# Reading the moving operand from the last token to the first in a two-layer decoder trunk

## The chip, the core and the metric

The kernel runs on one core of a Trainium2 chip. A core has a matrix engine (TensorE; PE in the profile, with its weight loads as PEld), a vector engine (VectorE, DVE), a scalar engine (ScalarE, ACT), GpSimd (POOL) and a sync engine (SyncE, SP) that here issues most of the DMAs. Data are worked on in an on-chip memory of 128 partitions (SBUF); TensorE writes its products into a second one (PSUM) of eight banks, each of 512 f32 per partition. The metric is the device time of one execution in microseconds; lower is better.

A matmul here has a *stationary* operand, a block of up to 128 x 128 that is loaded into the array by a weight load of its own, and a *moving* operand, which is streamed past it column by column. Each column of the moving operand gives one column of the output.

## What is computed

A trunk of two layers over 256 tokens with 1024 features. Each layer has a SwiGLU feed-forward of half weight, a token mixer (differential attention in the first layer, forgetting attention in the second), and another feed-forward. Before each stands an RMS norm whose shift and scale come from a conditioning vector.

```python
def swiglu(h, w_in, w_out):
    g, u = jnp.split(h @ w_in, 2, axis=-1)
    return (jax.nn.silu(g) * u) @ w_out

for layer in range(DEPTH):
    if layer == N_A_LAYERS:
        k_sh, v_sh, F_sh = shared_kv(x, ...)
    mod = c_act @ ada_w[layer] + ada_b[layer]
    sh1, sc1, g1, sh2, sc2, g2, sh3, sc3, g3 = jnp.split(mod, N_MOD, axis=-1)
    h = modulate(rms_norm(x, norm_g[layer, 0]), sh1, sc1)
    x = x + 0.5 * g1[:, None, :] * swiglu(h, ffn_w_in[layer, 0], ffn_w_out[layer, 0])
    h = modulate(rms_norm(x, norm_g[layer, 1]), sh2, sc2)
    mix = diff_attention(h, ...) if layer < N_A_LAYERS else forgetting_attention(h, ..., k_sh, v_sh, F_sh)
    x = x + g2[:, None, :] * mix
    h = modulate(rms_norm(x, norm_g[layer, 2]), sh3, sc3)
    x = x + 0.5 * g3[:, None, :] * swiglu(h, ffn_w_in[layer, 1], ffn_w_out[layer, 1])
return rms_norm(x, final_g)
```

The hidden width of the feed-forward is 2816. All inputs and outputs are f32.

## The kernel before, in words

The data are kept transposed: features on the partitions, tokens along the free dimension. So nearly every projection is a product whose *weights are stationary* (a block of 128 input features by 128 output features) and whose *moving operand is the data* (128 input features by 256 tokens). The output in PSUM is 128 output features by 256 tokens.

Full f32 accuracy is made from a faster format, f32r, by splitting each number into a high part (the value rounded to f32r) and a low part (what is left). Weights become `wh` and `wl`, data `HH` and `HL` (in the feed-forward's hidden layer `hidh` and `hidl`; in the attentions' outputs `oh`, `ol`, `obh`, `obl`). One product of a 128 x 128 block is then three matmuls into the same place of PSUM: `wh` with the high data, `wl` with the high data, `wh` with the low data. The function `mm3` (L405) issues these three; every projection with stationary weights calls it:

- the up projections of the feed-forwards, with outputs `pf` (the first blocks of the very first one), `pg` and `pu` (gate and up halves);
- the down projections of the first three feed-forwards, output `po`;
- the projections right after a down projection, whose moving operand is 258 columns wide (`SX`, L33): 256 tokens and the columns of the shift, since the norm's factor is not known yet and is multiplied in later (outputs `lp`, `lq`, `lg`, `lu`);
- the queries and keys of the first attention (`pqk`), some keys of the second (`pk`), and the output projections of the attentions (`pw` with `oh`, `ol`, `obh`, `obl`).

Not through `mm3` go the value projections (`pv`, where the data are stationary and the weights move), the down projection of the last feed-forward (`Last.down`, also with moving weights; its output is named `po` too, but its rows name the weights first), the scores, the transposes and the value products of the attentions (`s`, `sb`, `wa`, `wb`, and a small `po`), and the sums of squares of the norms (`psn`, in plain f32).

Weights come from HBM in pieces of 128 x 1024 (`raw`), loaded by SP; ACT rounds each piece to `wh`, and DVE subtracts to get `wl`. The tile of such a piece is 1088 wide (`WB`, L35), and at the first pieces of some stages the piece is put 16 or 32 elements further into it (`shift`, L263 to L270).

The order on each engine is that of the program's text. The class `InOrder` (L54) wraps each engine's calls: it keeps a rough clock of its own for each engine and uses it only to decide, while the program is built, where on ACT and DVE a piece of weights is prepared between other work. To know when an operand is ready, it keys each operand by its tensor's name and, for some tensors, by the offset of the view (L81).

Of the kernel before, what the change touches and what calls it, by code (L numbers as in the profile page):

```python
# [50 lines left out]
V_ADAB = 65  # L51


class InOrder:  # L54


# [18 lines left out]
    def __getattr__(self, name):  # L75
        f = getattr(self.engine, name)

        def call(*args, **kw):
            aps = [v for v in (*args, *kw.values()) if hasattr(v, "tensor")]
            if aps:  # L80
                names = [(v.tensor.name, v.offset if v.tensor.name[:2] in ("HH", "HL", "x_", "mo") else 0) for v in aps]  # L81
                cost = self.fixed + self.rate * math.prod(aps[0].shape[1:])
                if aps[1:] and aps[1].dtype == F32:
                    cost *= {"matmul": 4, "transpose": 2}.get(name, 1)
                start = max(InOrder.ready.get(n, 0.0) for n in names[name == "matmul":])
                if self.fill and not self.busy:
                    self.busy = True
                    self.fill(start)
                    self.busy = False
                self.t = max(self.t, start) + cost  # L90
                if name == "dma_start":
                    InOrder.ready[names[0]] = self.t + 2.0
                else:
                    outs = [names[0]] + ([(kw["accum_out"].tensor.name, 0)] if kw.get("accum_out") is not None else [])
                    for n in outs:
                        InOrder.ready[n] = self.t + 0.06
            else:
                self.t += 1.3
            return self.tc.keep_in_program_order(f(*args, **kw))  # L99
        return call  # L100
# [3 lines left out]
def trunk(ctx, tc, a, out):  # L104
# [243 lines left out]
    def work(cols):  # L348

        credit[0] = min(CREDIT, credit[0] + pace[0] * 2 * cols / 2048)  # L350
        if mode[0] != "hold":
            bg()
# [51 lines left out]

    def mm3(ps, w, xx, first, last):  # L405
        (wh, wl), (xh, xl) = w, xx
        mm(ps, wh, xh, start=first, stop=False, skip_group_check=True)
        mm(ps, wl, xh, start=False, stop=False, skip_group_check=True)
        mm(ps, wh, xl, start=False, stop=last, skip_group_check=True)
        work(P)  # L410


    HH = cp_.tile([P, NC, SP_], F32R, name="HH")
    HL = cp_.tile([P, NC, SP_], F32R, name="HL")
# [89 lines left out]
    def late_pair(src, dst, r, name):  # L504

        banks = [mmbank(f"{name}{b}") for b in range(2)]
        blk = take(src)
        for k in range(NC):
            for b in range(2):
                mm3(banks[b][:, :SX], blk(k * 256 + b * P), hx[k], k == 0, k == NC - 1)  # L510
            if k == NC - 1:
                late_out(dst, banks, r)
            yield k, NC

    def late_pairs(src, dsts, m, then):

        pb = []
        for i in range(2):  # L520
            banks = [mmbank(f"lp{i}{b}") for b in range(2)]
            pb.append(banks)
            blk = take(src)
            for k in range(NC):
                for b in range(2):
                    mm3(banks[b][:, :SX], blk(k * 256 + b * P), hx[k], k == 0, k == NC - 1)
                if i == 0:
                    if k == 3:
                        r = rstd_of(then)
                        mh = MakeH(r, m) if m else None  # L530
                else:
                    if k == 0:
                        late_out(dsts[0], pb[0], r)
                    if mh:
                        mh.go()
        if mh:
            mh.go(9 - mh.k)
        late_out(dsts[1], pb[1], r)
        mode[0] = "run"
        return r  # L540


    def ffn(l, i, kind, m, nxt, at=2):
# [24 lines left out]
        if (l, i) == (0, 0):  # L568
            banks = ([mmbank(f"pf{b}") for b in range(4)] + [sbank(f"pf{b}") for b in range(4, 6)]
                     + [abank("pf6"), bbank("pf7")])  # L570
            for k in range(NC):
                if k:
                    ada_block()
                    cp_part()
                    ada_block()
                f = make_h(k, kind, m)
                sub_part()
                cp_part()
                f()
                sub_part()  # L580
                blk = take("win0")
                for b in range(4 * K0):
                    mm3(banks[b // 2][:, (b % 2) * 256:(b % 2) * 256 + 256], blk(b * P), hn[k],
                        k == 0 and b % 2 == 0, k == NC - 1)
# [915 lines left out]
```

## Time and profile before

| | us |
|---|---|
| median of two runs | 977.47 |
| the two runs | 976.68 and 978.26 |
| span of the profiled execution (first to last instruction) | 974.4 |

The profiled execution's own time is given as its span only; the 3.1 us between the span and the median of the runs lie outside the program's first and last instruction, or in the difference between executions. In the profile an engine's busy time is the union of its instructions' times. A matmul's own duration (276 ns for 256 columns) is longer than the step from one matmul to the next, since matmuls overlap in the array; the pace is read from the starts, or from the length of a stretch divided by the number of matmuls in it. Nearly all instructions carry the line L99, since `InOrder` records them; the tiles' names tell them apart. Out<-in names an instruction's output and inputs.

The DMA queues moved 268.22 MB at 275 GB/s on average; DVE is busy for 818.5 us and ACT for 552.4 us.

### The profile page before, as it was taken

How to read it: one execution, taken by the hardware profiler on the slowest of the kernel's cores; microseconds unless marked ns; L12 is line 12 of the kernel's file. 1: busy time of each engine (PE TensorE's matmuls, PEld its weight loads, DVE VectorE, ACT ScalarE, POOL GpSimd, SP SyncE). 2: the span in 40 equal slices, each digit the busy share in tenths (PEclk: the TensorE clock that was granted, in tenths of full speed). 3: DMA queues.
4: the chain of work that ended last, by engine and by line, in shares of the span. 5: the costliest groups of instructions: out<-in, count | busy, mean ns of one | idle time of the engine just before them, and what ended most of it. 6: DMA issues, size and time to landing. Idle time of an engine off the chain costs nothing.

```text
span 974.4 us, 20491 instructions
## 1 busy us (share of the span) xinstructions
PE 963.7 (99%) x8124; PEld 939.9 (96%) x8124; DVE 818.5 (84%) x1372; ACT 552.4 (57%) x902; POOL 54.6 (6%) x94
## 2 busy tenths in 40 slices
PE   8999999999999999999999999999999999999997
PEld 6999999998999999999997999999998999999997
DVE  7989979989999999878899989989977699555575
ACT  5466545566787645455576554445567576455432
POOL 0000200000112000000000000000011014300000
PEclk9999999999999999999999999999999999999999
DMA  9988999967776699888959899998885337978651
GB/s 360 415 352 279 332 372 339 345 225 272 293 239 232 209 381 370 293 287 314 329 179 370 308 338 337 345 314 319 297 278 174 104 109 228 266 149 276 185 152 44
DMA packets 69473, 268.22 MB, mean 275 GB/s; under 512 B 9417, under 2 KB 10225, under 8 KB 59266
## 3 DMA queue, kind: packets, MB, share of 16 engines
q1 hardware_dynamic: 66016, 259.69, 76.1%
q0 software_dynamic: 3072, 6.92, 2.5%
q8 instruction: 63, 1.03, 0.4%
q10 hardware_dynamic: 290, 0.32, 0.1%
q14 instruction: 32, 0.26, 0.1%
HBM read 264.75 MB, written 2.66 MB: 274 GB/s over the span
## 4 chain that ended last, share of the span: by engine, by line
PE 97%; DVE 1%; DMA 1%; ACT 0%; issue 0%; SPq 0%; DVEq 0%; ACTq 0%
PE po L99 25%; PE pg L99 21%; PE pu L99 21%; PE pf L99 5%; PE pv L99 5%; PE pw L99 4%; PE lp L99 4%; PE pqk L99 3%; PE wb L99 1%; PE lq L99 1%; PE lu L99 1%; PE lg L99 1%; PE pk L99 1%; PE sb L99 1%; DMA ada<-in_ada 1%; PE s L99 1%
## 5 line engine op out<-in xcount | busy, mean ns | idle before, releaser
L99 ACT CAST wh<-raw 128x1024 fp32r<-128x1024 f32 (+1 forms) x360 | 347.3, 975 | 210.8 <-PE pu L99 82.0
L99 DVE TENSOR_TENSOR wl<-raw,wh 128x1024 fp32r<-128x1024 f32 (+1 forms) x360 | 398.6, 1126 | 70.9 <-ACT sg L99 20.3
L99 DVE CUSTOM_DVE_ANT_0 ada<-ada,cact,vecs 128x1024 f32<-128x1024 f32 x160 | 203.6, 1279 | 0.4 <-DMA ada<-in_ada 0.4
L99 PE MATMUL pg<-HH,wh 128*128 128x256 f32 x608 | 168.0, 276 | 0.0
L99 PE MATMUL pg<-HH,wl 128*128 128x256 f32 x608 | 167.9, 276 | 0.0
L99 PE MATMUL pu<-HH,wh 128*128 128x256 f32 x608 | 167.9, 276 | 0.0
L99 PE MATMUL pu<-HL,wh 128*128 128x256 f32 x608 | 167.9, 276 | 0.0
L99 PE MATMUL pg<-HL,wh 128*128 128x256 f32 x608 | 167.9, 276 | 0.0
L99 PE MATMUL pu<-HH,wl 128*128 128x256 f32 x608 | 167.9, 276 | 0.0
L99 PE MATMUL po<-hidh,wh 128*128 128x256 f32 x528 | 145.7, 276 | 0.0
L99 PE MATMUL po<-hidh,wl 128*128 128x256 f32 x528 | 145.7, 276 | 0.0
L99 PE MATMUL po<-hidl,wh 128*128 128x256 f32 x528 | 145.7, 276 | 0.0
L99 PEld LDWEIGHTS pg<-HH,wh 128*128 128x128 f32 x608 | 114.1, 188 | 0.7 <-issue 0.6
L99 PEld LDWEIGHTS pg<-HH,wl 128*128 128x128 f32 x608 | 114.1, 188 | 0.0
L99 PEld LDWEIGHTS pu<-HH,wh 128*128 128x128 f32 x608 | 114.1, 188 | 0.0
L99 PEld LDWEIGHTS pg<-HL,wh 128*128 128x128 f32 x608 | 114.1, 188 | 0.0
L99 PEld LDWEIGHTS pu<-HL,wh 128*128 128x128 f32 x608 | 114.1, 188 | 0.0
L99 PEld LDWEIGHTS pu<-HH,wl 128*128 128x128 f32 x608 | 114.1, 188 | 0.0
L99 PEld LDWEIGHTS po<-hidh,wh 128*128 128x128 f32 x528 | 99.1, 188 | 0.0
L99 PEld LDWEIGHTS po<-hidl,wh 128*128 128x128 f32 x528 | 99.1, 188 | 0.0
L99 PEld LDWEIGHTS po<-hidh,wl 128*128 128x128 f32 x528 | 99.1, 188 | 0.0
L99 ACT CAST hidh<-hf 128x512 fp32r<-128x512 f32 x44 | 27.3, 621 | 40.5 <-DVE hf L99 40.4
(226 smaller groups left out, 1848.4 us busy)
## 6 DMA issues: line engine op xcount, KB each, us to landing
raw<-in_win SPq DMA_DIRECT2D x176, 512.0 KB, 6.8
ada<-in_ada SPq DMA_DIRECT2D x79, 1024.0 KB, 7.2
raw<-in_wout SPq DMA_DIRECT2D x48, 384.0 KB, 5.3
raw<-in_wout SPq DMA_DIRECT2D x48, 320.0 KB, 5.5
raw<-in_wqk SPq DMA_DIRECT2D x16, 512.0 KB, 5.8
raw<-in_wo SPq DMA_DIRECT2D x16, 512.0 KB, 5.8
raw<-in_wlast SPq DMA_DIRECT2D x16, 512.0 KB, 4.5
raw<-in_wv SPq DMA_DIRECT2D x8, 512.0 KB, 7.2
```

The costliest lines, as they stand in the source:

```text
L99: return self.tc.keep_in_program_order(f(*args, **kw))
```

## The change

In `mm3`, the view of the output and both views of the data are turned: they start at the last column and step by -1. So the last token is streamed first, and its output column is written first, into the same place as before. The stationary operands stay as they are. In `InOrder` the offset that keys an operand is replaced by that of the lowest element that the view touches, which gives the same key for a turned view as for a straight one.

```diff
+def lowest(v):
+
+    return v.offset + sum(step * (n - 1) for step, n in v.ap[1:] if step < 0)
+
+
+def turned(v):
+
+    return v[:, ::-1]
...
-                names = [(v.tensor.name, v.offset if v.tensor.name[:2] in ("HH", "HL", "x_", "mo") else 0) for v in aps]
+                names = [(v.tensor.name, lowest(v) if v.tensor.name[:2] in ("HH", "HL", "x_", "mo") else 0) for v in aps]
...
     def mm3(ps, w, xx, first, last):
         (wh, wl), (xh, xl) = w, xx
+        ps, xh, xl = turned(ps), turned(xh), turned(xl)
         mm(ps, wh, xh, start=first, stop=False, skip_group_check=True)
         mm(ps, wl, xh, start=False, stop=False, skip_group_check=True)
         mm(ps, wh, xl, start=False, stop=last, skip_group_check=True)
```

The order of the instructions is the same on every engine. What differs, beside line numbers, are waits of TensorE on its own semaphore (PE_49) at sixteen products: `lp00`, `lp01`, `lp10` and `lp11` at each of three places, and `pg1` and `pu1` at each of two. On TensorE, at the end of the first down projection, the rows before are (names of output, data and weights; the semaphores waited for in brackets):

```order
L99 MATMUL po7_2450<-hidl10_1760,wh_2405 128x256
L99 MATMUL lp00_2569<-HH_92,wh_2429 128x258 [waits Activation_49]
L99 MATMUL lp00_2569<-HH_92,wl_2456 128x258 [waits DVE_49]
L99 MATMUL lp00_2569<-HL_93,wh_2429 128x258 [waits DVE_49]
L99 MATMUL lp01_2570<-HH_92,wh_2429 128x258
```

Now they are:

```order
L109 MATMUL po7_2450<-hidl10_1760,wh_2405 128x256
L109 MATMUL lp00_2569<-HH_92,wh_2429 128x258 [waits PE_49,Activation_49]
L109 MATMUL lp00_2569<-HH_92,wl_2456 128x258 [waits DVE_49]
L109 MATMUL lp00_2569<-HL_93,wh_2429 128x258 [waits DVE_49]
L109 MATMUL lp01_2570<-HH_92,wh_2429 128x258 [waits PE_49]
```

Nothing moved; two of the five products got a wait. Waits of this kind stood at other products before, too, for example where the same down projection goes on to its second output tile:

```order
L99 MATMUL po0_1746<-hidl10_1760,wh_1683 128x256
L99 MATMUL po1_1847<-hidh0_733,wh_1713 128x256 [waits PE_49]
L99 MATMUL po1_1847<-hidh0_733,wl_1750 128x256
L99 MATMUL po1_1847<-hidl0_734,wh_1713 128x256
L99 MATMUL po1_1847<-hidh0_733,wh_1713 128x256
```

There, the wait is for the bank's earlier user, and nothing of it differs after the change.

## The prediction

> **What bounds the kernel now.** I read the page first: its busy times, the row of slices with TensorE's granted clock, and the chain of work that ended last.
>
> ```profile
> PE 963.7 (99%) x8124; PEld 939.9 (96%) x8124; DVE 818.5 (84%) x1372; ACT 552.4 (57%) x902; POOL 54.6 (6%) x94
> PEclk9999999999999999999999999999999999999999
> PE 97%; DVE 1%; DMA 1%; ACT 0%; issue 0%; SPq 0%; DVEq 0%; ACTq 0%
> PE po L99 25%; PE pg L99 21%; PE pu L99 21%; PE pf L99 5%; PE pv L99 5%; PE pw L99 4%; PE lp L99 4%; PE pqk L99 3%; PE wb L99 1%; PE lq L99 1%; PE lu L99 1%; PE lg L99 1%; PE pk L99 1%; PE sb L99 1%; DMA ada<-in_ada 1%; PE s L99 1%
> ```
>
> TensorE is busy for 99% of the span at the full granted clock, and 97% of the chain is its own work. So a nanosecond more or less per product goes straight into the time, as many times as there are products. A busy share does not say how fast the products follow each other, however: matmuls overlap in the profile. I take that from stretches of the chain in order of time, which hold nothing but products of one kind. The columns are start, length, what and how many.
>
> ```profile
> 20.54 5.74 PE pf L99 x48
> 137.96 59.84 PE po L99 x528
> 201.13 8.70 PE lp L99 x72
> ...
> 317.90 0.73 PE lu L99 x6
> 318.63 0.71 PE pg L99 x6
> ...
> 320.77 0.71 PE pu L99 x6
> 321.48 0.68 PE pg L99 x6
> ```
>
> The down projection of a feed-forward runs 528 products of 256 columns in 59.84 us: 113.3 ns each, not one gap. The up projections run at the same 0.68/6 = 113.3 ns, apart from their first block of weights: 0.71/6 = 118.3 ns. The very first feed-forward runs much of its time at 5.74/48 = 119.6 ns, with the same shape of product. The products with 258 columns (256 tokens and two columns for the shift) take 8.70/72 = 120.8 ns. So one shape has two paces, about 113 and 118 to 120 ns, each held for dozens of products. [...]
>
> How many products change is read from the groups of instructions by form (name, weights' shape, moving shape, count).
>
> ```profile
> L99 PE MATMUL pg<-HH,wh 128*128 128x256 f32 x608 | 168.0, 276 | 0.0
> L99 PE MATMUL po<-hidh,wh 128*128 128x256 f32 x528 | 145.7, 276 | 0.0
> L99 PE MATMUL pf<-HH,wl 128*128 128x256 f32 x128 | 35.8, 280 | 0.2 <-DVE wl L99 0.2
> L99 PE MATMUL lp<-HH,wh 128*128 128x258 f32 x96 | 27.8, 289 | 0.0
> L99 PE MATMUL pqk<-HH,wh 128*128 128x256 f32 x96 | 27.0, 282 | 0.0
> L99 PE MATMUL pw<-obh,wh 128*128 128x256 f32 x64 | 18.4, 288 | 0.0
> L99 PE MATMUL lg<-HH,wh 128*128 128x258 f32 x32 | 9.4, 295 | 0.0
> L99 PE MATMUL pk<-HH,wh 128*128 128x256 f32 x32 | 8.8, 276 | 0.0
> ```
>
> Each name stands three times (weight high part with both halves of the data, weight low part with one); pu is like pg, lu and lq are like lg, and pw has a second group of 64 with the other attention's data. With 256 columns that is 3 x (2 x 608 + 528 + 128 + 96 + 2 x 64 + 32) = 6384 products; with 258 columns 3 x (96 + 3 x 32) = 576. So 6960 of the 8124 matmuls turn round. The last down projection (the po rows whose weights stand second in the product), the values and the attention's own products keep their direction.
>
> **The change part by part.** *What moves.* Nothing: the same products stand in the same order on all five engines, and no DMA is added or moved past another. The recording layer's names still agree, since the new helper gives a turned view the offset of its lowest element. Cost of this part 0; no cover is needed, since no instruction is added that would need one.
>
> *The added waits.* Sixteen products, where a stage takes over the banks of the one before (the lp banks, and pg1 and pu1), get a wait on TensorE's own earlier work, for the bank's last user, tiles ago. The po stretch above has the same kind of wait before the change (at its second output tile, shown with the change) and no gap: 59.84 us for 528 products. Lower end 0. Upper end: the product in front must finish first, 276 ns long instead of 113.3 ns to the next start, so 163 ns x 16 = 2.6 us. I take 0, since the awaited writer is dozens of products back. Behind such a wait only the next products queue; DVE and ACT would wait for the bank by the same amount.
>
> *The turned reading and writing.* This is the only real term, and no row of this kernel shows a descending stream on the moving side. I bound it per product.
>
> The lower end comes from products with fewer moving elements behind the same 128-column weights:
>
> ```profile
> 744.53 0.61 PE L99 MATMUL wb<-vb,wtb 128*128 128x64 f32 x4
> 744.98 0.60 PE L99 MATMUL wa<-tri,d 128*128 128x128 f32 x4
> 745.42 0.38 PE L99 MATMUL wb<-tri,d 128*128 128x128 f32 x2
> ```
>
> From one start to the next: four matmuls of 64 columns in 0.45 us (112.5 ns), four of 128 columns in 0.44 us (110 ns). So with less to stream a matmul still does not come faster than 110 ns, and 113.3 ns is already close to what the weight loads allow. A gain of the direction cannot exceed 3.3 ns on 6384 products (21.1 us) and 10.8 ns on the 576 wide ones (6.2 us): 27.3 us in all.
>
> The upper end comes from a matmul of the same 256 columns in plain f32, between two wide products in the normalization:
>
> ```profile
> 200.53 0.59 PE L99 MATMUL psn<-acc,ones 128*128 128x256 f32 x2
> 200.78 0.47 PE L99 MATMUL lp<-HH,wh 128*128 128x258 f32 x1
> 201.09 0.28 PE L99 MATMUL lp<-HH,wl 128*128 128x258 f32 x1
> ```
>
> From 200.53 to 201.09 us stand two psn matmuls (one product in plain f32 takes two) and one lp: (560 - 121)/2 = 220 ns per psn, about twice the pace. If a descending stream moved one element where an ascending one moves two, a product would cost this: (220 - 113.3) x 6384 + (220 - 120.8) x 576 = 681 + 57 = 738 us more.
>
> Between -27 and +738 us I take 0. All the data are still read and written in adjacent addresses, 256 in a row, the same bytes in the same rows and banks; only the sign of the step differs. psn reads its data in ascending order as well and differs in the number format; so the nearest rows are those of the same format and shape, and these stand at 113.3 ns. Nothing behind the product depends on which token comes first: ACT and DVE wait for a whole bank.
>
> [...]
>
> *The sum* is against the profiled span of 974.4 us: 0 + 0 + 0. The median of the runs is 977.47 us, 3.1 us above that span, and I carry that over: 977.5 us.
>
> **The rivals.** *Half pace (slower).* Every turned product at 220 ns: 977.5 + 738 = 1715 us. [...] Against it: adjacent addresses, as above. [...] It decides as soon as a turned product costs 2.8 ns more, since 2.8 x 6960 = 19.5 us is 2% of the time, about what a measurement of this kernel can tell from no change.
>
> *The slower rhythm (slower).* Turned, the stream meets the next weight load differently, and the products lock into the pace of the first feed-forward. 119.6 - 113.3 = 6.3 ns on the 6384 less the 384 pf products: 6.3 x 6000 = 38 us, so 1015 us; if only half of the stretches fall into it, 997 us. For it: both paces exist now for one shape, and a block of weights that starts elsewhere is enough to change them (0.71 against 0.68 us at 318 to 321 us). Against it: after that seam the rhythm finds back to 113.3 ns within five groups.
>
> *The faster rhythm (faster).* Weight load and stream disturb each other less, and products come down to 110 ns: 977.5 - 27.3 = 950 us. Against it: those 110 ns need every stretch at the best matmul seen. Then DVE would be late next in places; in the first down projection it is already busy for 54.12 of 59.84 us:
>
> ```profile
> 137.96:197.80 59.84, 59.84 (x531) 59.84 (x530) 54.12 (x84) 35.03 (x52) 0.00 (x0) 1.00 0.96 351
> 908.04:968.03 59.99, 59.97 (x528) 59.77 (x527) 41.83 (x72) 21.78 (x24) 0.00 (x0) 1.00 0.41 124
> ```
>
> *It does nothing at all because it is not done* is no rival here: the access patterns of the built instructions do carry a step of -1.
>
> **How the numbers follow.** No change of pace 0.52 (970 to 985 us, its own range: the added waits above, a seam or two in another rhythm on either side). Slower rhythm 0.16, of which 0.12 beyond 2%. Faster rhythm 0.12, of which 0.05 beyond 2%. Half pace, or a good part of it, 0.20. So faster 0.05, slower 0.12 + 0.20 = 0.32, the same 0.63. The first three cases hold 0.80, and the range spans them: from 950 us, the floor of the fast rhythm, to 1020 us, the slow rhythm with the waits. The half pace is left out above it.
>
> **What would show it.** The po stretches of 528 products should again last 59.8 us; at half pace they would last 528 x 0.220 = 116 us, in the slow rhythm 63 us, in the fast one 58 us. The last down projection (second row of the windows above, 59.99 us) is not turned and should keep its time in any case: it is the control. A slowdown that is the same per product in pg, po and lp speaks for the memory pace, one that differs from stretch to stretch for the rhythm. Gaps of 0.1 to 0.2 us at the sixteen seams would show the added waits. The prediction is wrong if a turned product's pace differs from 113.3 ns by 2.8 ns or more over most of the stretches.

## The result, and the profile after

The changed kernel takes 1002.41 us (median of two runs, 1002.02 and 1002.81) against 977.47 us before: a ratio of 1.0257, 95% interval 1.0228 to 1.0287. It is slower. The span of its profiled execution is 1000.8 us, 26.4 us longer than before.

The page of the changed kernel, its busy times and the shares of the chain that ended last:

```profile
PE 991.3 (99%) x8124; PEld 968.4 (97%) x8124; DVE 820.6 (82%) x1372; ACT 553.8 (55%) x902; POOL 55.1 (6%) x94
PE 97%; DVE 1%; ACT 1%; issue 0%; DVEq 0%; ACTq 0%
```

TensorE is still 99% busy with the same 8124 matmuls, so the 26.4 us are not a wait: the matmuls themselves follow each other more slowly. The chain of the changed kernel in order of time (start, length, what, how many) says by how much:

```profile
142.90 62.19 PE po L109 x528
208.39 8.64 PE lp L109 x72
439.82 62.19 PE po L109 x528
502.00 2.88 PE lp L109 x24
675.14 62.19 PE po L109 x528
934.34 60.04 PE po L109 x528
```

The first three down projections take 62.19/528 = 117.8 ns per product, where they took 113.3. The fourth, which is not turned, takes 60.04 us as against 59.99: the control holds. The lp products follow the po stretch at 439.82 without a gap (439.82 + 62.19 = 502.01), so the added wait at that seam costs nothing that can be seen. The products of 258 columns became a little quicker, 8.64/72 = 120.0 ns as against 120.8.

The up projections of the second feed-forward run from their first pg group to the po stretch. Before and after, from the same view:

```profile
318.63 0.71 PE pg L99 x6
...
427.56 59.84 PE po L99 x528
```

```profile
326.70 0.72 PE pg L109 x6
327.42 0.72 PE pu L109 x6
...
439.11 0.71 PE pu L109 x6
439.82 62.19 PE po L109 x528
```

That is 427.56 - 318.63 = 108.93 us before and 439.82 - 326.70 = 113.12 us after, for 960 matmuls: 4.4 ns more for each. With 4.45 ns on the 3648 up products and the 1584 down products, 5232 x 4.45 = 23.3 us of the 26.4 us lie in the feed-forwards. About 1 us more lies in the first attention's queries and keys, where stretches of 48 products take 5.66 us instead of 5.46. About 2 us lie ahead of and in the `pf` products, and those are not the direction's: 382 of them take 47.60 us here and 45.87 us before, but 45.90 us in the read-only kernel below, which turns them too.

The engines behind TensorE only wait longer. ACT's longest wait, for a weight tile to come free:

```profile
ACT wh L109 <- PE pu L109: 110.5, 76, 2.5
```

It was 82.0 us before.

### The profile page after: what moved, and what is told of

Same layout as the page of the kernel before. It is cut to its first block, busy times and chain, and to the rows that moved or that the text cites. A ratio compares the mean times of both kernels' runs of the same rounds, so it can differ in the third digit from the quotient of the medians.

```text
span 1000.8 us, 20496 instructions
## 1 busy us (share of the span) xinstructions
PE 991.3 (99%) x8124; PEld 968.4 (97%) x8124; DVE 820.6 (82%) x1372; ACT 553.8 (55%) x902; POOL 55.1 (6%) x94
## 4 chain that ended last, share of the span: by engine, by line
PE 97%; DVE 1%; ACT 1%; issue 0%; DVEq 0%; ACTq 0%
PE po L109 25%; PE pg L109 21%; PE pu L109 21%; PE pf L109 5%; PE pv L109 4%; PE pw L109 4%; PE lp L109 3%; PE pqk L109 3%; PE wb L109 1%; PE lq L109 1%; PE lu L109 1%; PE lg L109 1%; PE pk L109 1%; PE sb L109 1%; PE s L109 1%; PE psn L109 1%
## 5 line engine op out<-in xcount | busy, mean ns | idle before, releaser
L109 PE MATMUL pg<-HL,wh 128*128 128x256 f32 x608 | 171.5, 282 | 0.0
L109 PE MATMUL pu<-HL,wh 128*128 128x256 f32 x608 | 171.5, 282 | 0.0
L109 PE MATMUL pg<-HH,wh 128*128 128x256 f32 x608 | 171.4, 282 | 0.0
L109 PE MATMUL pu<-HH,wh 128*128 128x256 f32 x608 | 171.3, 282 | 0.0
L109 PE MATMUL po<-hidl,wh 128*128 128x256 f32 x528 | 148.9, 282 | 0.0
L109 PE MATMUL po<-hidh,wh 128*128 128x256 f32 x528 | 148.4, 281 | 0.0
L109 PE MATMUL po<-hidh,wl 128*128 128x256 f32 x528 | 147.8, 280 | 0.0
L109 PE MATMUL po<-wl,hidh 128*128 128x256 f32 x176 | 48.7, 276 | 0.0
```

## The experiments

I call the 16 elements by which the first weight piece of a stage is shifted in its tile the *shift*. Two theories stood first. R: the direction of *reading* sets the pace. W: *writing* PSUM backwards costs it. Then there was the question whether the two paces belong to the two directions, or are rhythms into which either direction can fall. The kernels a3, a4, b1 to b4, c1 and c2 ran once each: their time is that of one execution, and their pace is read from its profile.

### Reading alone, writing alone

a1_read_only:

```diff
-        ps, xh, xl = turned(ps), turned(xh), turned(xl)
+        xh, xl = turned(xh), turned(xl)
```

> The data are read from the last token to the first, but the output is written straight (so tokens come out in the wrong places, and the attentions work on reordered tokens; the amount of work is the same). Theory R (the direction of reading, where the stream meets the next weight load, sets the pace): like the changed kernel, po stretches of 528 products 62.2 us, about 1002 us. Rival W (writing PSUM backwards costs it): po stretches 59.84 us, about 977 us. Both in part: a pace between 113.3 and 117.8 ns.

a2_write_only:

```diff
-        ps, xh, xl = turned(ps), turned(xh), turned(xl)
+        ps = turned(ps)
```

> The data are read straight, but the output is written from the last column to the first (again tokens come out in the wrong places). Theory R: like the kernel before, po stretches 59.84 us, about 977 us. Rival W: po stretches 62.2 us, about 1002 us.

Measured: reading alone 1001.55 us, ratio to the kernel before 1.0253 (1.0238 to 1.0268); writing alone 976.99 us, ratio 1.0003 (0.9994 to 1.0013). The chain of the read-only kernel, then that of the write-only kernel:

```profile
140.82 62.19 PE po L109 x528
437.74 62.19 PE po L109 x528
673.07 62.19 PE po L109 x528
932.27 60.04 PE po L109 x528
```

```profile
137.90 59.84 PE po L109 x528
427.50 59.84 PE po L109 x528
655.96 59.84 PE po L109 x528
```

The whole price lies in the reading. Writing the columns of a bank in falling order costs nothing that can be measured. W falls.

### Does the shift choose the pace?

a3_straight_no_kick, the kernel before with `shift[first] = 0` in place of 16:

> The kernel before, with the 16 elements by which the first weight piece after a seam is shifted taken away in all four feed-forwards (the last down projection keeps its own). If the pace is a rhythm that the shift selects and the direction only changes which rhythms there are: the feed-forwards stay at 117.8 to 120 ns, po stretches 62 to 63.3 us, 1000 to 1012 us in all. If the two paces belong to the two directions alone: po stretches 59.84 us and 977 us, the shift does nothing.

a4_turned_other_kicks, the changed kernel with other shifts:

```diff
-        shift[first] = 16
+        shift[first] = {(0, 0): 32, (0, 1): 48, (1, 0): 8, (1, 1): 24}[l, i]
```

> The changed kernel, with shifts of 32, 48, 8 and 24 elements in place of 16 in the four feed-forwards, one each. If a rhythm of 113.3 ns exists for the turned direction too and 16 elements only fail to reach it: at least one of the po stretches or one of the pg/pu stretches goes down to 113.3 ns per product (po 59.84 us). If the turned direction has no such rhythm: all stay at 117.8 ns or go to 120 ns (po 62.2 to 63.4 us), 1000 to 1012 us.

Measured: 975.91 us for the straight kernel without the shift (the kernel before, beside it: 976.13 to 977.27 us), the po stretches through `mm3` 59.84 us; 1001.81 us for the turned one with other shifts, the po stretches that it turns 62.19 us. In these two runs the shift decided nothing. My idea that a well-chosen shift would bring the turned direction to 113.3 ns got no support, and four shifts were tried.

### Which streams pay, and how much of it is the stream

b1_weights_turned, the kernel before, with the weights read backwards where they are the moving operand (and the outputs written so):

```diff
-                wh, wl = w
+                wh, wl = turned(w[0]), turned(w[1])
+                po = turned(po)
...
-                        mm(banks[t], hh[:, ts], wh, start=k == 0, stop=False)
...
+                        bt = turned(banks[t])
+                        mm(bt, hh[:, ts], turned(wh), start=k == 0, stop=False)
...
```

> The kernel before, with only those products turned that it streams weights in (the value projections, 512 columns, and the last down projection, 256 columns). If the price belongs to any backward-read stream (theory R): the last down projection goes from 113.3 to 117.8 ns per product, 59.99 to 62.2 us, and the products of 512 columns from some 230 ns to 235 ns (a price at the ends of a stream) or 239 ns (a price per column). If it belongs to the data tiles and where they lie beside the weights: the last down projection keeps 60.0 us. The po stretches of the first three stay at 59.84 us in both.

Measured: 979.94 us. The chain before, three stretches of 512-column products; then the chain of this kernel, with the third and the last down projection:

```profile
225.97 8.26 PE pv L99 x36
512.25 8.40 PE pv L99 x36
524.58 11.19 PE pv L99 x48
```

```profile
226.38 8.40 PE pv L104 x36
513.10 8.40 PE pv L104 x36
525.48 11.40 PE pv L104 x48
656.69 59.84 PE po L104 x528
909.17 62.25 PE po L104 x528
```

The last down projection, until now the control, goes to 62.25 us, while the others stay. So the price is not bound to the data's tiles. A product of 512 columns pays (8.40 - 8.26)/36 = 3.9 ns, or (11.40 - 11.19)/48 = 4.4 ns: about the same as one of 256, so the price does not grow with the columns. But not every stream pays. One stretch takes 8.40 us turned and took 8.40 us straight: it stood at the slower pace already, 233 ns, before anything was turned. That looks like a choice between two paces, and not like something added to each backward stream.

b2_turned_widths and b3_straight_widths, the changed kernel and the kernel before with fewer columns in some of the up projections:

```diff
-                        mm3((pg, pu)[b // 2][:, (b % 2) * 256:(b % 2) * 256 + 256],
-                            blk(kk * 512 + b * P), hn[k], k == 0 and b % 2 == 0, k == NC - 1)
+                        wd = (256, 240, 224, 192)[2 * l + i] if k else 256
+                        mm3((pg, pu)[b // 2][:, (b % 2) * 256:(b % 2) * 256 + wd],
+                            blk(kk * 512 + b * P), (hn[k][0][:, :wd], hn[k][1][:, :wd]), k == 0 and b % 2 == 0, k == NC - 1)
```

> The changed kernel with fewer columns in the gate and up products of three feed-forwards: 256, 240, 224 and 192 of the 256 tokens in the first to fourth, from the second input block on (the left-out columns lack those blocks). If the backward stream itself is longer (P): 117.8 ns at 256, and the pace falls with the columns, to about 111 ns at 240 and the weight loads' 110 to 112 ns at 224 and 192. If the backward stream holds up the weight load beside it (Q): 240 and 224 columns still take 115 to 118 ns, and 192 stays above 112 ns.

> The kernel before with the same fewer columns. If the stream sets the pace of 113.3 ns: down to the weight loads' 110 to 112 ns at 240 columns and no lower at 224 and 192. If the weight load beside it does: 113.3 ns at every width.

Measured: 985.08 us turned, 978.36 us straight. The chain of the turned kernel in its second feed-forward (240 columns; every eighth input block has 256):

```profile
345.57 0.67 PE pu L109 x6
346.24 0.71 PE pg L109 x6
346.95 0.71 PE pu L109 x6
347.66 0.67 PE pg L109 x6
```

At 240 columns and below both directions run at 0.67/6 = 111.7 ns, which 16 or 48 columns fewer don't improve: windows of 20 us hold 180, 180 and 181 matmuls at 240, 224 and 192 columns, in both kernels. I take that for the pace of the weight loads alone, an estimate from these counts; it is the same for both directions. A weight load held up by a backward stream, as expected under Q, would have shown at 240 columns too. The widths fit P, a backward stream that takes longer and that the weight load hides at 240 columns. They don't show that it is the stream itself that is longer, since forward streams took the same 117.8 ns too, as the straight kernel shows.

These are its windows for the second and the third po stretch (TensorE's matmuls in 50 us, with two or three that reach in from before):

```profile
430.00:480.00 50.00, 50.00 (x427) 50.00 (x426) 2.86 (x6) 0.00 (x0) 1.00 0.87 304
660.00:710.00 50.00, 50.00 (x444) 50.00 (x443) 2.88 (x6) 0.00 (x0) 1.00 0.89 315
```

The second, entered from products of 240 columns, ran at 117.8 ns from end to end, read straight and with 256 columns: 50 us/117.8 ns = 424 products. The third, with the same kind of instructions but entered from products of 224 columns, ran at 113.3 ns: 441. So the straight direction has both paces.

c2_turned_ends, the changed kernel with just a few columns fewer:

```diff
+                        c0, c1 = ((0, 254), (0, 252), (0, 248), (8, 256))[2 * l + i] if k else (0, 256)
```

> The changed kernel with slightly fewer columns in the gate and up products, from the second input block on: tokens 0 to 253 in the first feed-forward, 0 to 251 in the second, 0 to 247 in the third, 8 to 255 in the fourth (the left-out columns lack those blocks). If the stream's length sets the turned pace column by column: 117 ns at 254, 116 ns at 252, 114.4 ns at 248, the same for both sets of 248. If the pace goes in steps with the memory's rows: 117.8 ns or 113.3 ns at these widths, with no value between that lasts, and the two sets of 248 may differ.

Measured: 994.77 us. The chain in the third feed-forward, where 248 columns are streamed backwards, after a block of 256:

```profile
570.99 0.71 PE pu L109 x6
571.70 0.68 PE pg L109 x6
572.38 0.68 PE pu L109 x6
```

248 columns take 0.68/6 = 113.3 ns backwards, what 256 take forwards, and the same at either end of the row (0 to 247 or 8 to 255). At 254 columns nothing is gained, and at 252 a part: in windows of 20 us in the first to fourth feed-forward there stand 171, 174, 178 and 178 products. Neither expectation fits fully: the pace does not fall column by column, and 252 gives a value between the steps.

The last down projection, which is read forwards in this kernel as in the changed one, shows the slower pace here, 62.22 us instead of 60.04, although its own weight pieces are shifted as before:

```profile
924.35 62.22 PE po L109 x528
```

### Where the stream begins

b4_turned_offset8, the changed kernel with the normalized data 8 elements further into their rows:

```diff
-    hn = [(HH[:, k, :S], HL[:, k, :S]) for k in range(NC)]
+    hn = [(HH[:, k, 8:8 + S], HL[:, k, 8:8 + S]) for k in range(NC)]
```

(`hx` and the columns of the norm's shift likewise.)

> The changed kernel with the normalized data placed 8 elements (32 bytes) further into their rows; the hidden layer's tiles stay. If the place where a stream begins within the memory's rows sets the pace: pg and pu (and lp, pqk, pf) get another pace than 117.8 ns, the po stretches keep 62.2 us. If the direction alone does: 117.8 ns in both, about 1002 us.

Measured: 1002.1 us, 117.8 ns in the moved up projections and in the unmoved down projections. For the backward streams this offset does not matter. It matters in a place that the expectation did not name. In the value projections (`pv`) the normalized data are the stationary operand, and the weights stream past them forwards. First the changed kernel, then this one:

```profile
233.19 8.26 PE pv L109 x36
```

```profile
232.32 8.40 PE pv L109 x36
```

That is the 8.40 us that the same stretch took in b1, where its stream was turned. Here nothing of it is turned; only its stationary blocks lie 32 bytes further. So in this run the place of the stationary operand did to a forward stream what backward reading does.

### Both directions in one kernel

c1_mixed gives each of the three matmuls of `mm3` a direction of its own; of the last two lines the first stands in the up projections and the second in the down projections:

```diff
+    def mm3(ps, w, xx, first, last, back=(0, 0, 0)):
+        (wh, wl), (xh, xl) = w, xx
+        for n, (w_, x_) in enumerate(((wh, xh), (wl, xh), (wh, xl))):
+            p_, x_ = (turned(ps), turned(x_)) if back[n] else (ps, x_)
+            mm(p_, w_, x_, start=first and n == 0, stop=last and n == 2, skip_group_check=True)
...
+    ((1, 0, 0), (0, 1, 0), (0, 0, 1), (b % 2,) * 3)[2 * l + i])
...
+    ((n >= 4,) * 3, (n < 4,) * 3, (k % 2,) * 3)[2 * l + i])
```

> Both directions in one kernel. The gate and up products: in the first feed-forward only the first of the three matmuls of a product is turned, in the second only the second, in the third only the third, in the fourth every other whole product. The first down projection is straight for four output tiles and then turned, the second turned for four and then straight, the third alternates from product to product. If a turned matmul has a fixed price of 4.45 ns: 114.8 ns where one of three is turned, 115.6 ns where half are, and in the first two down projections a step from 113.3 to 117.8 ns and from 117.8 to 113.3 ns at the middle, at once. If both paces are rhythms that hold once they are entered: the first down projection keeps the 113.3 ns of its straight half when it turns, and the second keeps 117.8 ns when it becomes straight. If the turned direction cannot hold the faster rhythm but the straight one can hold either: the first steps to 117.8 ns, the second keeps 117.8 ns.

Measured: 1000.89 us. Windows of 25 us within the po stretches: straight half and turned half of the first, turned half and straight half of the second, and the alternating third.

```profile
145.00:170.00 25.00, 25.00 (x223) 25.00 (x222) 1.44 (x3) 0.00 (x0) 1.00 0.92 338
176.00:201.00 25.00, 25.00 (x215) 25.00 (x214) 1.44 (x3) 0.00 (x0) 1.00 0.92 330
442.00:467.00 25.00, 25.00 (x214) 25.00 (x213) 1.44 (x3) 0.00 (x0) 1.00 0.86 294
473.00:498.00 25.00, 25.00 (x223) 25.00 (x223) 1.44 (x3) 0.00 (x0) 1.00 0.92 324
676.00:701.00 25.00, 25.00 (x215) 25.00 (x214) 1.44 (x3) 0.00 (x0) 1.00 0.87 317
```

Within one stretch, on the same tiles, the pace steps with the direction: 223 products in 25 us when straight, 214 or 215 when turned (two or three of each count reach in from before). The straight half of the second stretch came down to 113.3 ns by itself, with no shifted weight piece at that place, so neither theory of a pace that holds once it is entered fits. It is no fixed price per turned matmul either. The chain in the first feed-forward's up projections, where one matmul in three is turned:

```profile
88.23 0.72 PE pg L109 x6
88.95 0.72 PE pu L109 x6
```

One turned matmul in three should have cost 114.8 ns by a fixed price. It costs 120.0 ns if it is the first or the second, and 117.8 ns if it is the third (windows of 25 us in the second and third feed-forward hold 210 and 214 matmuls). Every other product turned costs as much as all of them: 215 in 25 us, in the fourth's up projections as in the third po stretch above. Each mixture lands on one of few values, 113.3, 117.8 or 120.0 ns.

### A version that beats both?

c3_best: straight, no shift, and only the products of 258 columns turned (120.0 ns instead of 120.8).

```diff
+        if xh.shape[1] == SX:
+            ps, xh, xl = turned(ps), turned(xh), turned(xl)
...
-        shift[first] = 16
+        shift[first] = 0
```

> A try at a version faster than both: the kernel before without the 16-element shift, and only the products of 258 columns turned (120.0 instead of 120.8 ns). From a3 the missing shift saves some 1.0 us (four seams of 48 to 96 products at 116 instead of 113.5 ns), the 576 products save 0.5 us: 975.4 us. If entering the feed-forwards from a turned stretch brings the slower rhythm into them: 980 to 1000 us.

Measured: 989.01 us, from 987.39 to 1000.34 over six runs, ratio 1.0103 (1.0062 to 1.0144). Its profiled execution, the slowest of them, shows straight po stretches in the slower rhythm, behind turned lp products or not:

```profile
141.19 62.19 PE po L109 x528
437.55 62.19 PE po L109 x528
672.82 62.19 PE po L109 x528
931.93 59.99 PE po L109 x528
```

d1_kick_back is the same with the shift of 16 put back.

> The kernel of c3_best with the 16-element shift at the four seams put back: straight, with only the products of 258 columns turned. In c3_best the straight feed-forwards ran at 117.8 ns. If the shift is what brings a straight stretch from the slower rhythm into the faster one: the first block of weights at about 116 ns, then 113.3 ns in all feed-forwards, po stretches 59.84 us, 976.3 us (0.5 us under the kernel before). If the shift does nothing and c3_best was slow because of the turned stretches ahead: po stretches of 62.2 us in the feed-forwards that follow a turned stretch, 987 to 1000 us.

Measured: 977.04 us, ratio 1.0004 (0.9995 to 1.0013). Its chain:

```profile
138.06 59.84 PE po L109 x528
201.21 8.64 PE lp L109 x72
427.55 59.84 PE po L109 x528
655.94 59.84 PE po L109 x528
```

So the shift has a use after all. The two kernels differ in it alone: with it all eleven executions took 976.47 to 979.79 us and the profiled one holds the faster rhythm; without it all six took 987.39 us or more. (They ran on different chips; the kernel before had medians of 978.15 us beside c3_best and 976.94 us beside d1.)

What picks the rhythm where the shift is missing is not shown. Up to the first lp products a3 and c3_best run the same instructions. In a3 the pf products ran at 119.6 ns to their end (the last 46 in 5.50 us), and the 672 up products behind them took 77.12 us (60.73 to 137.85); in c3_best 382 pf products took 45.94 us and the 672 up products 80.09 us (61.10 to 141.19), 4.4 ns more for each. So a stretch does not simply keep the pace that it finds. The first stage of c3_best was slow before any turned product had run, so the slower rhythm needs no turned stretch ahead of it.

The half microsecond that the 258-column products gained in d1 is lost again in other straight products: the 96 pk products take 11.31 us (10.90 before) and a stretch of 72 pw products 8.57 us (8.29). No version that ran more than once beat the kernel before; a3's single 975.91 us was not repeated.

## Why the prediction was right or wrong

**The bound** was read rightly: TensorE's pace carries straight through to the time (busy for 99% of the span before and after, and the span 26.4 us longer).

**The count** held: 6960 matmuls are turned, the last down projection is not and kept its 60 us.

**The added waits** were taken as 0, with 2.6 us as the upper end. The seam after a po stretch has no gap, and the first pg and pu groups of the second feed-forward take 0.72 us as against 0.71 before. Right, as far as these seams show.

**The writing** was taken as free, and that is shown (ratio 1.0003).

**The reading** is the step that failed: "Between -27 and +738 us I take 0", with the reason that only the sign of the step differs. The sign is not free. A backward stream of 256 columns takes 117.8 ns where a forward one took 113.3, and no run had it at 113.3 ns. So the likeliest case, 977.5 us, did not come, and the forecast of no change was wrong by 25 us. It is wrong by the prediction's own sign as well: 4.45 ns over most of the stretches is more than the 2.8 ns named there. The price is far from the upper end of 738 us, too. That end rests on a stream that moves one element in place of two, at the 220 ns of the psn rows, and no run shows such a stream: the turned products took 117.8 ns with 256 columns and 120.0 ns with 258. That the weight loads set the lower end, 110 ns, was an estimate; with fewer columns the pace stood at 111.7 ns (b2, b3).

**The rivals.** The slower rhythm came, with a chance of 0.16 and a time of 1015 us. Its sign and its place (every long stretch of turned 256-column products outside pf) held; its price was mis-sized. It was taken from the first feed-forward's 119.6 ns, while the rhythm is 117.8: 4.45 ns and not 6.3, so 26.7 us on the same 6000 products and not 38. (The spans differ by 26.4 us, of which some 2 us are not the direction's.) The row that it was taken from stands for the pf products, and these varied between runs: read forwards, 382 of them took 45.87 us before (120.1 ns) and 46.79 us in b3 (122.5 ns). The trace of before held the better row: 0.71/6 = 118.3 ns, right behind a seam. What I called its mechanism is right in part. The straight direction does have two rhythms, 113.3 and 117.8 ns, and both can last for a whole stretch (b3); how the stream meets the weight load no run shows. But turned products did not fall into the slower one by accident: with five shifts, one offset and different stretches ahead, no wholly turned stretch of 256 columns held the faster one.

**The range**, 950 to 1020 us, took this in because it was drawn out to the slower rhythm, a case with a chance of 0.16. The central reasoning, that the direction is free, failed; that the time still lies within the range is owed to a side case whose price was too high, and in that sense to luck.

**What stays open.** Why a backward stream keeps to the slower rhythm is not settled. Excluded by runs are the writing (a2), the data's tiles as the cause (b1) and a fixed price per turned matmul (c1). An offset of 8 elements did not change it (b4; other offsets were not tried), and a weight load that is held up at every width does not fit (b2, b3). But the weight side has a part: the place of a stationary operand changed the pace of forward streams in b4 (pv) and in d1 (the shift). What the values 113.3, 117.8 and 120.0 ns come from can't be seen in a profile. Whether the price hangs on the direction of the weight load beside the stream was not tried.

## What to carry to other kernels

When one engine is busy for 99% of the time, measure its pace in stretches of equal instructions before and after: 4.45 ns on 113.3 is invisible in a busy share and made this kernel 2.6% slower. The same matmuls had more than one steady pace here (113.3 and 117.8 ns), so a term that "changes nothing" deserves the price of the next slower pace, taken from the row of the same shape. And read the moving operand forwards in a stream like this one: backwards, its 256 columns held 113.3 ns in no run; the direction of writing made no difference (a2, ratio 1.0003).

## What the runs showed of the hardware that was not expected

- Reading the moving operand backwards costs 3.9 to 4.5 ns per matmul of 256 or 512 columns where the forward stream ran in the faster of its two paces (b1, after), nothing where it ran in the slower one already (b1: 8.40 us for 36 matmuls both ways), nothing at 240 columns and below (111.7 ns both ways, b2 and b3), and 248 columns backwards take the 113.3 ns of 256 forwards (c2).
- Writing PSUM backwards cost nothing that can be measured (a2, ratio 1.0003).
- The same straight products ran at 113.3 ns or at 117.8 ns for a whole stretch of 528 (b3, c2, c3_best); with 16 elements of shift in the first weight piece of a stage they stood at 113.3 ns (d1), though c2's last stretch was slow with its shift in place.
- Stationary data 8 elements further took a forward stream of 512 columns from 8.26 to 8.40 us for 36 matmuls (b4), as turning it did (b1).
- One backward matmul in a group of three cost more than three, if it was the first or the second: 120.0 against 117.8 ns per matmul (c1).
- The time of one kernel can move with this: c3_best took 987 to 1000 us, and the kernel before, run beside it on the same chip, 976.56 to 984.43 us. One feed-forward in the slower rhythm would be (1056 + 528) x 4.45 ns = 7.0 us; those runs were not profiled, so that this is what happened in them is an estimate.
